# A two-layer hybrid attention and state-space block: the order of fetches and of the first products in the opening

## The chip, the cores and the metric

The kernel runs on one core of a Trainium2 chip. The metric is the device time of one execution in microseconds (us). The engines named below are PE (TensorE, matrix products and transposes), DVE (VectorE), ACT (ScalarE), POOL (GpSimd) and SP (SyncE, which only issues DMAs).

## The reference, cut to what matters

Two layers are applied to 1024 latent tokens and 256 context tokens of width 1024. Only the head of the first layer is touched by the change:

```python
mod = silu(c) @ w_mod[l] + b_mod[l]              # six vectors of 1024: shift, scale, gate, twice
h  = rms_norm(x, norm1_g) * (1 + sc1) + sh1      # and the same for the context with c_ctx
... = split(h @ w_in)                            # q, kv, z, xbc, dt, window q/k/v
```

The rest of a layer is a latent attention, a bidirectional state-space scan, a windowed attention, an output product, and a gated MLP. The scan takes `ssm_dt_bias`, `ssm_a_log` and `ssm_d`, and the windowed attention takes `swa_sink`. These are the scan and sink parameters of the change; each is a handful of numbers that is spread over 128 partitions.

## The kernel before, in words

Everything is kept as features by tokens: `x[f]` holds 128 features (block f of 8) for 1280 tokens. The tokens come in three chunks, 0 and 1 of 512 latent tokens and 2 of 256 context tokens. Every float32 product is split in a high and a low part of each operand (`wh`, `wl` of a weight; `hhi`, `hlo` of the normed input), so that one product of a block with a weight is three matmuls; the first weight has only 64 columns and takes two, so the three first weights together take eight matmuls per block and chunk.

The opening (`start`, from line 1783) does these things for layer 0:

- `fetch(q)` (line 1793) loads the rows of chunk q, one 512 KB DMA for 128 tokens. `turn(q, ...)` (line 1824) transposes them on PE into `x`, 4 transposes for a block of a 512-token chunk, with a copy out of PSUM on DVE or ACT alternately. `stat(q)` takes the mean squares on ACT, and `spread(q, dg)` multiplies them out over the partitions on PE into `pn`.
- `mods(0, (n,), ...)` (line 303) makes 512 columns of `c @ w_mod`; columns 0 and 2 serve the first half of the features (blocks 0 to 3), columns 1 and 3 the second half (blocks 4 to 7). Each column loads four 512 KB pieces `wm` (line 317), does 16 matmuls into `pm`, copies it out (`ev`, line 368), transposes it (`pt`) and reduces it to `modT` (lines 374 and 376). It is a generator that is advanced by hand: the first `next` issues its four loads, two more do the matmuls, the last one the rest.
- `load_params(0, ...)` (line 260) loads ten small parameter arrays as rows (`ra`, `rb`), on ACT's queue, then transposes them on PE (`pa`) into `prm`, and loads five broadcasts `sm` on POOL's queue (lines 281 to 286). Setup puts two more small DMAs of ones (`kpd`, `oned`, line 250) on POOL's queue. `load_params(1, ...)` does the same later in the program for layer 1, all on POOL's queue.
- `apply(q, half)` (line 1832, and `Norm.apply`, line 2105) norms and modulates four blocks of a chunk: for an even block DVE, ACT, DVE; for an odd block DVE, ACT, ACT, POOL.
- `first` (line 695) does the products of the three first weights. It walks six stretches, (chunk, blocks) = (0, 0 to 1), (0, 2 to 3), (1, 0 to 1), (1, 2 to 3), (0, 4 to 7), (1, 4 to 7), and calls `ahead(n)` before the n-th. The context chunk's products follow (`proj2`). The accumulators of the six sums of chunks 0 and 1 are five PSUM buffers of tag `f` (there are five) and one of tag `b` (three); `turn` takes an `f` for chunks 0 and 1, a `b` for chunk 2.

PE runs exactly in program order (`manual_schedule`, line 1950), and so the order of the calls above is the order of its work. The other engines and the DMA queues are ordered at compile time by a scheduler with a priority in program order; `tc.issue_after(ins)` forces what is traced in it behind `ins` on the same queue. Work of the `bg` kind is interleaved with a lower priority.

After the opening all eight `x[f]` are spilled to HBM (`xsp`, line 1980) and the pool that held them is closed. A new pool takes its memory, in which the background generator `mods_v` (line 336) makes the eight other columns of `c @ w_mod` on DVE: 16 instructions and two reductions a column. Its `wm` loads (line 347) can start only when the memory of the `x[f]` under them is free. The program then waits for that generator (`self.drain()` in `body`) before it goes on with the scan.

The lines that carry the order of the opening before:

```python
        dgs = {0: stat(0)}
        next(m[0]); fetch(1); next(m[2])
        turn(0, range(KT)); spread(0, dgs[0])
        next(prm, None); next(m[0]); next(m[0])
        dgs[1] = stat(1); turn(1, range(KT)); spread(1, dgs[1])
```

Of the kernel before, what the change touches and what calls it, by code (L numbers as in the profile page):

```python
# [9 lines left out]
F32 = mybir.dt.float32  # L10
# [9 lines left out]
KT = D // 128  # L20
# [3 lines left out]
NCH = NT // 128  # L24
# [90 lines left out]
class Emit:  # L115
# [92 lines left out]
    def setup(self):  # L208
        nc, tc, ctx = self.nc, self.tc, self.ctx
        self.C = ctx.enter_context(tc.tile_pool(name="const", bufs=1))  # L210
        self.DR = ctx.enter_context(tc.tile_pool(name="dram", bufs=1, space=DRAM))
        c = self.C
        self.ident = c.tile([128, 128], F32, name="ident")
        make_identity(nc, self.ident)
        self.identr = c.tile([128, 128], F32R, name="identr")
        nc.vector.tensor_copy(self.identr, self.ident)
        self.identb = c.tile([128, 128], BF16, name="identb")
        nc.vector.tensor_copy(self.identb, self.ident)
        self.ones = c.tile([128, 128], F32, name="ones")
        nc.vector.memset(self.ones, 1.0)  # L220

        self.negF = c.tile([128, 128], F32, name="negF")
        self.negB = c.tile([128, 128], F32, name="negB")
        for d, t in enumerate((self.negF, self.negB)):
            self.tri(t, d)
            nc.vector.tensor_scalar(out=t, in0=t, scalar1=-1.0, scalar2=-NEG, op0=ALU.add, op1=ALU.mult)

        self.mprev = c.tile([128, 128], BF16, name="mprev")
        self.mnext = c.tile([128, 128], BF16, name="mnext")
        nc.vector.tensor_copy(self.mprev, self.negF)  # L230
        nc.vector.tensor_copy(self.mnext, self.negB)
        self.eps = c.tile([128, 1], F32, name="eps")
        nc.vector.memset(self.eps, EPS)
        dr = lambda name, shape, dt=F32: self.DR.tile(shape, dt, name=name)
        self.spill = dr("xsp", [KT, 128, NT])
        self.fmd = dr("fmd", [NCH, 128, 7, 128])
        self.tmd = dr("tmd", [NCH, 128, 5, 128])
        self.zd = dr("zd", [NCH, 128, 3, 128])
        self.hbd = dr("hbd", [NCH, 128, 384])
        self.gd = dr("gd", [NF, 128, NT])  # L240
        self.ybd = dr("ybd", [3, 128, NT])
        self.acsd = dr("acsd", [12, NCH, 128])
        self.kd = [[dr(f"kd{i}{p}", [128, NT]) for p in range(2)] for i in range(3)]
        self.qd = [[dr(f"qd{i}{p}", [128, NT]) for p in range(2)] for i in range(3)]
        self.swd = [dr(f"swd{i}", [128, NT]) for i in range(4)]
        self.shd = {i: [dr(f"shd{i}{p}", [128, NT]) for p in range(2)] for i in (0, 2, 3)}
        self.kpd = [dr(f"kpd{p}", [33 - p, NT]) for p in range(2)]
        self.oned = dr("oned", [1, NT])
        for d in (self.kpd[0][32:33, :], self.oned):
            nc.gpsimd.dma_start(out=d.rearrange("o (a b) -> (o a) b", b=128), in_=self.ones[0:NCH, :])  # L250
        self.qpd = [[dr(f"qpd{t}{p}", [32 if t == 0 else 128, NT]) for p in range(2)] for t in range(2)]
        self.modd = [[dr(f"modd{l}_{p}", [4, 2, 16, 128]) for p in range(3)] for l in range(DEPTH)]

# [5 lines left out]

    def load_params(self, l, wtile):  # L260
        nc, I = self.nc, self.I
        q = nc.scalar if l == 0 else nc.gpsimd
        prm = self.C.tile([128, PC_ALL], F32, name=f"prm{l}")
        ra, rb = wtile([PC_A, 128], "ra"), wtile([PC_ALL - PC_A, 128], "rb")
        r = lambda ap: ap.rearrange("(f p) -> f p", p=128)
        for o, n, src in ((PC_N1, 8, r(I['norm1_g'][l])), (PC_N2, 8, r(I['norm2_g'][l])),
                          (PC_QN, 2, r(I['mla_q_norm_g'][l])), (PC_KVN, 1, r(I['mla_kv_norm_g'][l])),
                          (PC_CW, 21, I['ssm_conv_w'][l].rearrange("k (f p) -> (k f) p", p=128)),
                          (PC_CB, 7, r(I['ssm_conv_b'][l])), (PC_SN, 3, r(I['ssm_norm_g'][l])), (PC_BM, 48, r(I['b_mod'][l]))):
            q.dma_start(out=ra[o:o + n, :], in_=src)  # L270
        q.dma_start(out=rb[0:66, :], in_=I['ffn_conv_w'][l].rearrange("k (f p) -> (k f) p", p=128))
        q.dma_start(out=rb[66:88, :], in_=r(I['ffn_conv_b'][l]))
        self.prm.append(prm)
        sm = self.C.tile([128, 12 + 12 + 4 + 3], F32, name=f"sm{l}")
        self.small.append(sm)
        yield 15.0
        pa = self.b("pa")
        self.tr(pa[:, 0:PC_A], ra)
        self.tr(pa[:, PC_A:PC_ALL], rb)
        nc.vector.tensor_copy(prm, pa[:, 0:PC_ALL])  # L280
        nc.gpsimd.dma_start(out=sm[:, 0:12], in_=I['ssm_dt_bias'][l].rearrange("a b -> (a b)").partition_broadcast(128))
        nc.gpsimd.dma_start(out=sm[:, 12:24], in_=I['ssm_a_log'][l].rearrange("a b -> (a b)").partition_broadcast(128))
        nc.gpsimd.dma_start(out=sm[:, 24:28], in_=I['swa_sink'][l].partition_broadcast(128))
        dsk = I['ssm_d'][l].rearrange("(i two) -> two i", two=2)
        for hf in range(2):
            nc.gpsimd.dma_start(out=sm[64 * hf:64 * hf + 64, 28:31], in_=dsk[hf].partition_broadcast(64))


    def mod_stat(self):
# [1493 lines left out]
    def start(self):  # L1783

        nc, I, tc = self.nc, self.I, self.tc
# [7 lines left out]
        def fetch(q):  # L1793
            for k in range(CHUNKS[q][0] // 128, CHUNKS[q][1] // 128):
                rows[k] = self.u(shape=[128, D], name="xr")
                nc.sync.dma_start(out=rows[k], in_=row(k))
# [10 lines left out]
        def stat(q):  # L1807
            s, e = CHUNKS[q]
            k0, k1 = s // 128, e // 128
            sp = lambda w, name: self.u(shape=[128, w], name=name) if q else self.W.tile([128, D], F32, tag="wlo", name=self.nm(name))  # L1810
            junk, dg = sp(D, "junk"), sp(512, "dg")
            for k in range(k0, k1):
                nc.scalar.activation(junk, rows[k], AF.Square, accum_out=st[:, k:k + 1])
            self.rsqrt(r[:, k0:k1], st[:, k0:k1], D)
            self.diag(dg, r[:, k0:k1], k1 - k0)
            return dg
# [7 lines left out]
        def turn(q, fs):  # L1824
            s, e = CHUNKS[q]
            for f in fs:
                p = self.b("ptr") if q == 2 else self.f("ptr")
                for k in range(s // 128, e // 128):
                    self.tr(p[:, k * 128 - s:k * 128 - s + 128], rows[k][:, f * 128:(f + 1) * 128])
                (nc.scalar.copy if f % 2 or q == 2 else nc.vector.tensor_copy)(x[f][:, s:e], p[:, 0:e - s])  # L1830
# [5 lines left out]
            norm.apply(CHUNKS[q], pn[:, s:e], [4 * hf + f for f in fs])  # L1836

        norm.halves = set()
        prm = self.load_params(0, xw)
        next(prm)  # L1840
        dgs = {0: stat(0)}
        next(m[0])
        fetch(1)
        next(m[2])
        turn(0, range(KT))
        spread(0, dgs[0])
        next(prm, None)
        next(m[0])
        next(m[0])
        dgs[1] = stat(1)  # L1850
        turn(1, range(KT))
        spread(1, dgs[1])
        with tc.issue_after(self.last_w.ins):
            for i in range(3):
                self.wready.append(self.wload(*self.wspec.pop(0), pool=i == 2, stage=self.X.tile([128, KT, 128], F32, tag="ft", name=self.nm("w")) if i == 2 else None))
        next(m[0], None)
        next(m[2])
        next(m[2])
        next(m[2], None)
        for q in range(2):  # L1860
            apply(q, 0)
        next(m[1])
        next(m[3])
        with tc.issue_after(self.last_w.ins):
# [2 lines left out]
        def ahead(i):  # L1867

            if i == 2:
                for n in (1, 3):  # L1870
                    next(m[n])
                    next(m[n])
                dgs[2] = stat(2)
            if i == 3:
                for n in (1, 3):
                    next(m[n], None)
                apply(0, 1)
                turn(2, range(KT))
                spread(2, dgs[2])
                with tc.issue_after(self.last_w.ins):  # L1880
                    self.wready.append(self.wload(*self.wspec.pop(0), tile=lambda sh, tag, name: self.u(F32R, sh, name)))
                    self.wprime(2)
            if i == 4:
                apply(1, 1)
                apply(2, 0)
                apply(2, 1)
        return x, (norm.hi, norm.lo), ahead
# [339 lines left out]
```

## Time and profile before

| | |
|---|---|
| median of 3 runs | 3299.73 us (3297.24 to 3301.19) |
| the profiled execution, its own time | 3301.97 us |
| span from the first to the last instruction in it | 3300.3 us |
| mean granted TensorE clock | 0.957 of full |
| busy: PE, DVE, ACT, POOL | 93%, 65%, 39%, 19% of the span |
| DMA | 392 MB, mean 119 GB/s |

The profile is that of one execution, with the time of each instruction, what it waited for, and when each DMA landed. Times in it count from the start of the span. A row of a timeline gives the start, the length, the engine, the line, the operation, and what it writes and reads; an idle time before it stands in brackets with what ended it. "SPq" is SP's queue, where a DMA's row is its issue and not its transfer. The first 220 us, 6.7% of the span, are the part that the change touches.

### The profile page before, as it was taken

The numbers are of one execution on the slowest core, as the hardware profiler recorded it, in microseconds if no ns is written. First come the engines' busy times: TensorE is split into PE (matmuls) and PEld (weight loads), VectorE is DVE, ScalarE is ACT, GpSimd is POOL, SyncE is SP. The second block draws the span as 40 slices with busy tenths as digits, with TensorE's granted clock in tenths as the row PEclk, the third lists the DMA queues.
The fourth block names the chain that finished last, engine by engine and source line by source line (L and its number), as shares of the span: only waits on it lengthen the run. The fifth ranks groups of instructions, "written<-read, shape, count | busy, mean of one in ns | idle before, by whom it ended". The sixth has DMA issues, their size and how long they took to land.

```text
span 3300.3 us, 40044 instructions
## 1 busy us (share of the span) xinstructions
PE 3067.8 (93%) x15321; PEld 2408.6 (73%) x15321; DVE 2145.1 (65%) x3172; ACT 1275.9 (39%) x2203; POOL 614.6 (19%) x382
## 2 busy tenths in 40 slices
PE   7989878997989999997999999889999899999998
PEld 4878755554868888886888788755557678887887
DVE  5985887665385566558865634878563767776544
ACT  5334543343263343342211543543342544444212
POOL 2104633444100000000000303544452000000001
PEclk9989988998999999998999999888999999999999
DMA  8765665102202212236652345754113122225321
GB/s 266 231 185 150 213 217 155 40 14 96 93 29 71 79 59 71 77 102 242 198 157 67 129 117 160 226 179 122 41 52 102 45 77 87 85 83 185 112 74 64
DMA packets 348160, 392.42 MB, mean 119 GB/s; under 512 B 37138, under 2 KB 274339, under 8 KB 347968
## 3 DMA queue, kind: packets, MB, share of 16 engines
q1 hardware_dynamic: 347004, 389.62, 37.5%
q8 instruction: 121, 1.98, 0.2%
q0 software_dynamic: 704, 0.14, 0.1%
q14 instruction: 71, 0.58, 0.1%
q10 hardware_dynamic: 260, 0.10, 0.0%
HBM read 284.48 MB, written 104.01 MB: 118 GB/s over the span
## 4 chain that ended last, share of the span: by engine, by line
PE 76%; DVE 14%; DMA 5%; issue 2%; ACT 2%; POOL 1%; SPq 0%; DVEq 0%; ACTq 0%; POOLq 0%
PE p L143 33%; PE X L143 10%; PE Z L143 7%; PE s L143 6%; PE py L143 5%; PE pc L143 4%; PE V L143 3%; PE Y L143 3%; DVE wm L354 2%; DVE mx L1362 1%; DMA gr<-gd 1%; PE pm L143 1%; DVE hb L2153 1%; PE pn L143 1%; PE pst L143 1%
## 5 line engine op out<-in xcount | busy, mean ns | idle before, releaser
L143 PE MATMUL p<-gh,wb 128*128 128x512 f32 (+1 forms) x1760 | 508.2, 372 | 20.5 <-ACT gh L1744 20.5
L436 ACT CAST wb<-w 128x512 fp32r<-128x512 f32 x411 | 254.0, 622 | 571.4 <-PE p L143 282.3
L437 DVE TENSOR_TENSOR wb<-w,wb 128x512 fp32r<-128x512 f32 x411 | 281.2, 689 | 260.6 <-ACT wb L436 256.4
L143 PEld LDWEIGHTS p<-gh,wb 128*128 128x128 f32 x1760 | 322.4, 190 | 79.5 <-ACT gh L1744 23.8
L143 PE MATMUL X<-hb,wb 128*128 128x512 f32 x1512 | 360.4, 391 | 9.5 <-ACT hb L2152 4.6
L1572 DVE SCALAR_TENSOR_TENSOR x<-p,modT,x 128x512 f32<-128x512 f32 (+1 forms) x280 | 193.4, 695 | 231.9 <-PE p L143 231.6
L143 PEld LDWEIGHTS X<-hb,wb 128*128 128x128 f32 x1512 | 284.8, 189 | 70.9 <-ACT hb L2152 5.3
L143 PE MATMUL p<-gl,wb 128*128 128x512 f32 (+1 forms) x880 | 327.2, 372 | 2.6 <-DVE gl L1745 2.6
L143 PE MATMUL p<-hhi,wh 128*128 128x512 f32 (+1 forms) x792 | 292.6, 377 | 5.4 <-ACT z L648 3.1
L143 PE MATMUL p<-hlo,wh 128*128 128x512 f32 (+3 forms) x792 | 290.9, 368 | 1.9 <-DVE hlo L2123 1.0
L143 PE MATMUL p<-hhi,wl 128*128 128x512 f32 (+1 forms) x744 | 273.3, 367 | 3.6 <-DVE wl L424 3.1
L143 PE MATMUL Z<-hb,wb 128*128 128x512 f32 x1008 | 245.8, 393 | 8.7 <-ACT wb L436 4.4
L1446 ACT ACTIVATE P<-s 128x512 f32<-128x512 f32 x240 | 142.5, 598 | 239.9 <-PE s L143 234.1
L2075 POOL TENSOR_TENSOR acc<-acc,sq 128x512 f32<-128x512 f32 x24 | 32.9, 1374 | 1042.8 <-ACT sq L2074 1042.5
L143 PEld LDWEIGHTS Z<-hb,wb 128*128 128x128 f32 x1008 | 189.1, 189 | 49.4 <-ACT wb L436 4.6
L1453 POOL TENSOR_TENSOR acc<-acc,P 128x1024 f32<-128x1024 f32 x69 | 168.9, 2448 | 189.1 <-ACT P L1446 169.9
L143 PEld LDWEIGHTS p<-gl,wb 128*128 128x128 f32 x880 | 167.1, 190 | 32.8 <-DVE gl L1745 5.1
L143 PEld LDWEIGHTS p<-hhi,wh 128*128 128x128 f32 x792 | 152.1, 193 | 32.0 <-ACT z L648 4.0
L143 PE MATMUL py<-P,vt 128*64 128x512 f32 (+3 forms) x744 | 174.3, 584 | 0.0
L354 DVE SCALAR_TENSOR_TENSOR wm<-wm,mstat,wm 128x512 f32<-128x512 f32 x224 | 161.3, 752 | 19.8 <-DMA wm<-in_w_mod_dram 19.2
L143 PEld LDWEIGHTS p<-hlo,wh 128*128 128x128 f32 (+1 forms) x792 | 150.2, 190 | 25.4 <-DVE hlo L2123 1.7
L143 PEld LDWEIGHTS p<-hhi,wl 128*128 128x128 f32 x744 | 143.0, 192 | 28.4 <-DVE wl L424 4.4
(396 smaller groups left out, 5947.7 us busy)
## 6 DMA issues: line engine op xcount, KB each, us to landing
wm<-in_w_mod_dram SPq DMA_DIRECT2D x96, 512.0 KB
w<-in_ffn_w_up_dram SPq DMA_DIRECT2D x88, 512.0 KB
w<-in_ffn_w_down_dram SPq DMA_DIRECT2D x44, 512.0 KB
w<-in_w_in_dram SPq DMA_DIRECT2D x30, 512.0 KB
gd<-ft SPq DMA_DIRECT2D x22, 640.0 KB
gr<-gd SPq DMA_DIRECT2D x22, 640.0 KB
ab<-acsd SPq DMA_DIRECT2D x36, 384.0 KB
tm<-tmd SPq DMA_DIRECT2D x38, 320.0 KB
```

Source lines behind the costliest of these rows:

```text
L143: self.nc.tensor.matmul(out=out, lhsT=lhsT, rhs=rhs, start=start, stop=stop, **kw)
L354: nc.vector.scalar_tensor_tensor(out=acc[:, v, :], in0=w[:, i, :], scalar=c, in1=acc[:, v, :], op0=ALU.mult, op1=ALU.add)
L436: self.nc.scalar.copy(t[:, 0], raw)
L437: self.nc.vector.tensor_sub(t[:, 1], raw, t[:, 0])
L1362: nc.vector.tensor_reduce(out=m[:, j, s:s + 1], in_=p, axis=AXX, op=ALU.max)
L1446: nc.scalar.activation(P[:, q * 512:(q + 1) * 512], s, AF.Exp, scale=sc)
L1453: (nc.vector if kt in ((2, 4, 6, 8) if self.scan else (4, 7)) else nc.gpsimd).tensor_add(acc, acc, P)
L1572: self.nc.vector.scalar_tensor_tensor(out=t[:, s:e], in0=p[:, 0:e - s], scalar=self.mcol(l, v, m)[:, o:o + 1], in1=t[:, s:e], op0=ALU.mult ...
L2075: (nc.gpsimd if self.n[ch] < 6 else nc.vector).tensor_add(acc, acc, sq[:, :n])
L2153: nc.vector.tensor_sub(lo, raw, hi)
```

## The change

Setup no longer loads `kpd` and `oned`; layer 0's small parameters go on SP's queue in place of ACT's, and its five broadcasts wait behind a second `yield` and go on SP's queue too. In the opening, columns 0 and 2 are fetched directly behind chunk 0; then come the small parameters, the three first weights, and only then chunk 1. Chunk 1 is turned, and its first half normed, in `ahead(2)`, that is behind the products of chunk 0 with blocks 0 to 3. Columns 1 and 3 are finished in `ahead(4)`, the context chunk is turned in `ahead(5)`, and the five broadcasts, `kpd` and `oned` are issued there.

```diff
-        for d in (self.kpd[0][32:33, :], self.oned):
-            nc.gpsimd.dma_start(out=d.rearrange("o (a b) -> (o a) b", b=128), in_=self.ones[0:NCH, :])
...
-        q = nc.scalar if l == 0 else nc.gpsimd
+        q = nc.sync if l == 0 else nc.gpsimd
...
         nc.vector.tensor_copy(prm, pa[:, 0:PC_ALL])
-        nc.gpsimd.dma_start(out=sm[:, 0:12], in_=I['ssm_dt_bias'][l]...)
+        if l == 0:
+            yield
+        q.dma_start(out=sm[:, 0:12], in_=I['ssm_dt_bias'][l]...)
...
-        prm = self.load_params(0, xw)
-        next(prm)
         dgs = {0: stat(0)}
         next(m[0])
-        fetch(1)
         next(m[2])
+        prm = self.load_params(0, xw)
+        with tc.issue_after(self.last_w.ins):
+            next(prm)
+            for i in range(3):
+                self.wready.append(self.wload(...))
+            fetch(1)
         turn(0, range(KT))
         spread(0, dgs[0])
         next(prm, None)
-        next(m[0])
-        next(m[0])
-        dgs[1] = stat(1)
-        turn(1, range(KT))
-        spread(1, dgs[1])
-        with tc.issue_after(self.last_w.ins):
-            for i in range(3):
-                self.wready.append(self.wload(...))
-        next(m[0], None)
-        next(m[2])
-        next(m[2])
-        next(m[2], None)
-        for q in range(2):
-            apply(q, 0)
+        def columns(ns):
+            for n in ns:
+                next(m[n])
+                next(m[n])
+                next(m[n], None)
+        columns((0, 2))
+        apply(0, 0)
         next(m[1])
         next(m[3])
         with tc.issue_after(self.last_w.ins):
             fetch(2)
         def ahead(i):
             if i == 2:
-                for n in (1, 3):
-                    next(m[n])
-                    next(m[n])
+                dgs[1] = stat(1)
+                turn(1, range(KT))
+                spread(1, dgs[1])
+                apply(1, 0)
+            if i == 4:
+                columns((1, 3))
+                apply(0, 1)
                 dgs[2] = stat(2)
-            if i == 3:
-                for n in (1, 3):
-                    next(m[n], None)
-                apply(0, 1)
+                apply(1, 1)
+            if i == 5:
                 turn(2, range(KT))
                 spread(2, dgs[2])
                 with tc.issue_after(self.last_w.ins):
                     self.wready.append(self.wload(...))
                     self.wprime(2)
-            if i == 4:
-                apply(1, 1)
+                    next(prm, None)
+                    for d in (self.kpd[0][32:33, :], self.oned):
+                        nc.sync.dma_start(out=d.rearrange("o (a b) -> (o a) b", b=128), in_=self.ones[0:NCH, :])
                 apply(2, 0)
                 apply(2, 1)
```

## Rows read from the trace of the kernel before

**Rows 1.** The chain of waits, 190 to 235 us: shares by line

```profile
by line: DVE wm L354 39.5%; PE p L143 21.0%; DVE xbc L508 10.7%; issue 8.9%; DVE modT L361 5.3%; DVE wl L424 5.1%; PE pt L148 4.3%; PE pdt L148 2.7%; DVE wm L352 1.8%; PE pa L148 0.7%; DVE modT L362 0.5%; DVE a L390 0.3%; DVE edge L516 0.1%
```

**Rows 2.** Busy time by stretch: stretch, length, PE, PEld, DVE, ACT, POOL, PEclk, DMA share, GB/s

```profile
0.00:10.00 10.00, 1.23 (x3) 0.54 (x3) 1.62 (x10) 1.48 (x2) 6.76 (x18) 1.00 0.74 178
10.00:20.00 10.00, 4.47 (x20) 4.17 (x21) 1.45 (x3) 4.85 (x9) 1.49 (x3) 1.00 0.74 195
20.00:30.00 10.00, 7.62 (x36) 3.61 (x35) 3.23 (x6) 7.22 (x14) 0.00 (x0) 0.83 0.96 345
...
100.00:120.00 20.00, 20.00 (x105) 17.13 (x104) 20.00 (x28) 5.12 (x6) 6.42 (x3) 1.00 0.75 220
...
200.00:220.00 20.00, 8.95 (x51) 7.67 (x49) 20.00 (x38) 7.51 (x10) 5.20 (x10) 0.74 0.54 165
```

**Rows 3.** Timeline of VectorE, 60 to 140 us: start, us, instruction, idle before it

```profile
76.35 0.47 DVE L2120 SCALAR_TENSOR_TENSOR nt<-x,a,pn 128x256 f32<-128x256 f32 x1
...
84.19 0.41 DVE L2126 TENSOR_TENSOR nt<-x,pn 128x256 f32<-128x256 f32 x1
...
88.04 0.88 DVE L352 TENSOR_SCALAR wm<-wm,mstat 128x512 f32<-128x512 f32 x2 [1.12 <-DMA wm<-in_w_mod_dram]
```

**Rows 4.** Timeline of SP's queue, 0 to 120 us

```profile
62.41 9.30 SPq L1980 DMA_DIRECT2D xsp<-x  x8
...
84.29 0.38 SPq L347 DMA_DIRECT2D wm<-in_w_mod_dram  x1
```

**Rows 5.** Timeline of TensorE, 14 to 41 us

```profile
16.01 6.25 PE L148 MATMUL ptr<-ident,xr 128*128 128x128 f32 x29 [4.46 <-DMA xr<-in_x_dram]
23.98 1.12 PE L143 MATMUL pn<-dg,ones 128*128 128x512 f32 x2 [1.72 <-DVE dg L403]
...
25.03 0.24 PE L148 MATMUL pa<-ident,rb 88*128 88x88 f32 x1
25.20 3.56 PE L143 MATMUL pm<-wm,mstat 128*32 128x512 f32 x16
...
29.91 3.39 PE L148 MATMUL ptr<-ident,xr 128*128 128x128 f32 x29 [0.67 <-DMA xr<-in_x_dram]
...
34.86 1.92 PE L143 MATMUL pm<-wm,mstat 128*32 128x512 f32 x16
37.72 0.63 PE L148 MATMUL pt<-ident,ev 128*128 128x128 f32 x4 [0.93 <-DVE ev L368]
40.57 0.50 PE L143 MATMUL p<-hhi,wh 128*128 128x512 f32 x1 [2.23 <-ACT hhi L2122]
```

**Rows 6.** The chain of waits, 0 to 110 us, in order of time

```profile
46.26 7.10 PE p L143 x24
...
77.53 7.58 PE p L143 x32
```

**Rows 7.** SP's waits, 0 to 100 us: total, times, longest

```profile
SPq L317 <- DMA xr<-in_x_dram: 11.4, 4, 4.6
```

**Rows 8.** DMA queues, 0 to 200 us: packets, MB, share of 16 engines

```profile
q0 software_dynamic: 384, 0.04, 2.2%
```

**Rows 9.** Timeline of POOL, 0 to 14 us

```profile
1.37 0.76 POOL L281 DMA_DIRECT2D sm<-in_ssm_dt_bias_dram  x1 [0.36 <-issue]
...
6.36 0.58 POOL L281 DMA_DIRECT2D sm<-in_ssm_dt_bias_dram  x1
```

**Rows 10.** Busy time by stretch, columns as above, 26 to 28 us

```profile
26.00:28.00 2.00, 2.00 (x16) 0.39 (x8) 0.00 (x0) 1.95 (x4) 0.00 (x0) 0.50 1.03 409
```

**Rows 11.** Timeline of all engines, 46 to 50 us: one odd block of a normed half

```profile
46.68 0.68 DVE L2126 TENSOR_TENSOR nt<-x,pn 128x512 f32<-128x512 f32 x1
...
47.39 0.82 ACT L2127 ACTIVATE nt<-nt,modT,a 128x512 f32<-128x512 f32 x1 [1.56 <-DVE nt L2126]
...
48.24 0.62 ACT L2128 CAST hhi<-nt 128x512 fp32r<-128x512 f32 x1
...
48.94 1.50 POOL L2129 TENSOR_TENSOR hlo<-nt,hhi 128x512 fp32r<-128x512 f32 x1 [2.73 <-ACT hhi L2128]
```

More of the change, by code (lines that the diff above doesn't have):

```diff
@@ L280, in load_params @@
         nc.vector.tensor_copy(prm, pa[:, 0:PC_ALL])
-        nc.gpsimd.dma_start(out=sm[:, 0:12], in_=I['ssm_dt_bias'][l].rearrange("a b -> (a b)").partition_broadcast(128))
-        nc.gpsimd.dma_start(out=sm[:, 12:24], in_=I['ssm_a_log'][l].rearrange("a b -> (a b)").partition_broadcast(128))
-        nc.gpsimd.dma_start(out=sm[:, 24:28], in_=I['swa_sink'][l].partition_broadcast(128))
+        if l == 0:
+            yield
+        q.dma_start(out=sm[:, 0:12], in_=I['ssm_dt_bias'][l].rearrange("a b -> (a b)").partition_broadcast(128))
+        q.dma_start(out=sm[:, 12:24], in_=I['ssm_a_log'][l].rearrange("a b -> (a b)").partition_broadcast(128))
+        q.dma_start(out=sm[:, 24:28], in_=I['swa_sink'][l].partition_broadcast(128))
         dsk = I['ssm_d'][l].rearrange("(i two) -> two i", two=2)
         for hf in range(2):
-            nc.gpsimd.dma_start(out=sm[64 * hf:64 * hf + 64, 28:31], in_=dsk[hf].partition_broadcast(64))
+            q.dma_start(out=sm[64 * hf:64 * hf + 64, 28:31], in_=dsk[hf].partition_broadcast(64))
     def mod_stat(self):
@@ L1838, in start @@
         norm.halves = set()
-        prm = self.load_params(0, xw)
-        next(prm)
         dgs = {0: stat(0)}
         next(m[0])
-        fetch(1)
         next(m[2])
+        prm = self.load_params(0, xw)
+        with tc.issue_after(self.last_w.ins):
+            next(prm)
+            for i in range(3):
+                self.wready.append(self.wload(*self.wspec.pop(0), pool=i == 2, stage=self.X.tile([128, KT, 128], F32, tag="ft", name=self.nm("w")) if i == 2 else None))
+            fetch(1)
         turn(0, range(KT))
@@ L1847, in start @@
         next(prm, None)
-        next(m[0])
-        next(m[0])
-        dgs[1] = stat(1)
-        turn(1, range(KT))
-        spread(1, dgs[1])
-        with tc.issue_after(self.last_w.ins):
-            for i in range(3):
-                self.wready.append(self.wload(*self.wspec.pop(0), pool=i == 2, stage=self.X.tile([128, KT, 128], F32, tag="ft", name=self.nm("w")) if i == 2 else None))
-        next(m[0], None)
-        next(m[2])
-        next(m[2])
-        next(m[2], None)
-        for q in range(2):
-            apply(q, 0)
+        def columns(ns):
[5 more added lines that the diff above has]
+        apply(0, 0)
         next(m[1])
```

## The prediction

> **What bounds the kernel now.** The change touches the first 220 us alone, so I looked first for what ends that stretch. The chain of waits around its end is mostly DVE's: `mods_v`'s multiply-adds hold 39.5% of it [rows 1]. The busy times say the same: DVE is busy without a gap from 100 to 120 us and again from 200 to 220, where PE has fallen to 8.95 of 20 us because the program drains the background generator [rows 2]. So the end of the stretch is the start of `mods_v` plus a fixed amount of DVE work. That start is at 88.04 us, when its first `wm` has landed [rows 3]; the load was issued at 84.29 [rows 4], as the last normed blocks of the context chunk were read (84.19 [rows 3]). Hence the rule of this sum: **a us by which the last reading of `x` moves is a us of the whole kernel**, and nothing that happens earlier counts unless it moves that.
>
> Before that point two things rule. Up to 40.57 us, the first product [rows 5], it is the DMAs: they moved only 178 and 195 GB/s in the first two stretches of 10 us [rows 2], against 409 when nothing disturbed them [rows 10]. From then on it is PE's fixed order with little idle time: 24 products at 46.26 and 32 at 77.53 are single pieces of the chain [rows 6].
>
> 0.2% of the time, 6.6 us, is about what a measurement of this kernel can tell from no change.
>
> **The early fetches.** Before the first product the program now needs chunk 0, columns 0 and 2, the small parameters and three weights; chunk 1, 2.1 MB, moves behind them. When has the last piece of column 2 landed? It is the twelfth of 512 KB, 6.3 MB. At 409 GB/s from 2.2 us on that is 17.6 us; on the present curve (1.78 MB by 10 us, 1.95 more by 20, then 345 GB/s [rows 2]) it is 27.4. Two losses make the difference. The broadcasts on POOL's queue took 2.2% of 16 engines for 200 us, 4.4 us of each [rows 8]; half of that goes, because POOL issues layer 1's five directly behind layer 0's (6.36 against 1.37 us [rows 9]) and will issue them even sooner. And SP stood still for 11.4 us over four issues, each until one of the `xr` had landed [rows 7], though they don't share a buffer; I read that as a limit on DMAs in flight which ACT's ten small ones now help to fill. I take 22 us, near the middle, since one loss is halved and the other shrinks.
>
> The ten parameters queue behind that on SP. By the same limit the last three can be issued only once column 2 has landed: 1 us of issuing and 2 of latency (between nothing and 2.4, the 3.75 us of a lone `wm` from issue to use [rows 3, 4] less 1.3 for its data). So the parameters are there at 25 us. The Trainium skill, in "DMA: Bandwidth & Descriptors", section "Issuing engines are not separate DMA queues", says that all queues share the same 16 engines and that another issuing engine saves only the sequencer's time, usually small beside the transfer. By that the move to SP would cost nothing, and the sum below would be 3 us smaller; the 11.4 us of waiting in SP's own order speak against it here.
>
> **From the parameters to the first product.** On PE `pa` stands ahead of column 0, so all that follows waits for the parameters. `pa` takes 0.3 (0.24 for the second [rows 5]). Column 0 took 3.56 us for 16 matmuls with the granted clock at 0.50, its 1.2 GHz level, after PE had stood still before and behind the sums of chunk 0; column 2 took 1.92 at 2.4 GHz [rows 5, 10]. PE will again come from waiting, so 3.5 for the first. From the start of column 2's matmuls to the end of its transposes it was 3.5 us (34.86 to 38.35 [rows 5]); with no work between, both columns now run one after the other: 5.1 + 3.5. Then 2.2 from 38.35 to the first product at 40.57 [rows 5]. Sum: 25 + 0.3 + 5.1 + 3.5 + 2.2 = **36.1**, 4.5 us earlier than now. Three weights follow the parameters on SP and are there before that: they are 1.3 MB.
>
> **From the first product on.** A stretch of 32 products takes 7.58 us [rows 6]. An odd block's low part needs 0.68 + 0.82 + 0.62 + 1.50 on four engines in a row [rows 11], some 4.4 after `pn` as its first step waits behind the even block's, while the first even block is ready at 1.5 and its eight products take 1.9. So where PE comes straight from `pn`, it waits 1.0 for the second block: 8.6 for 32 products, and 10.1 from `pn`. Today this stall is paid once; three times now, since the norm of each half stands directly ahead of its products.
>
> - Chunk 0, blocks 0 to 3: 36.1 + 8.6 = 44.7. Now that end is 53.4 (46.26 + 7.10 [rows 6]): 8.7 gained.
> - Chunk 1 is turned there, in place of before the first product. It takes 3.39 with five PSUM buffers free, 6.25 for chunk 0 beside ACT's statistics [rows 5]. Three of the five `f` buffers now hold sums, so two are left: I take 4.8, the middle. Then `spread` 1.12 [rows 5] and a copy of 0.6: 51.2.
> - Chunk 1, blocks 0 to 3: 10.1, to 61.3.
> - Columns 1 and 3, one after the other: 3.5 each, 7.0, to 68.3. They now cost PE about that less 2 x 0.9 waiting for `ev`, beside products.
> - `modT`, and chunk 0, blocks 4 to 7: 2.2 to the first product, then 8.6, to 79.1. The second half of chunk 1 is normed under it.
> - The context is turned: half of 4.8, `spread` 1.0, to 82.5.
> - Its norm: 8.2 as now (76.35 to 84.60 [rows 3]), to **90.7** against 84.6.
>
> The last reading of `x` is then **6.1 us later**. What was gained at the start (8.7) is spent on turning chunk 1 behind the first products (6.5, which lay under the fetches before), on stalls on `pn` and `modT` that were filled with other products (about 6), and on `ev` (2).
>
> What is late next: the spill of `x` needs the turned context. Today its eight issues begin at 62.41 [rows 4], 22 us before the memory is wanted. In the new order they begin at about 80, and 5.24 MB at 409 GB/s are 12.8 us, so until 93; the first `wm`, issued at 91, would land at 94.2 anyway (91 + 3.75, less rounding). I add nothing, but 0 to 3 us is the bound if `wm` queues behind the spill.
>
> Costed at nothing: the five broadcasts, `kpd` and `oned` on SP (seven issues of some 0.4 us in a queue that is idle there, for values that are read after 200 us); the later second half of the parameters; statistics of chunk 1 on ACT, which waits for PE then. If ACT's order at compile time puts these ahead of a norm, up to 5 us come on top.
>
> Sum: 3299.7 + 6.1 = **3306** against the median; against the profiled execution's 3301.97, which stands 2.2 above the median, 3308.
>
> **The rivals.**
>
> - *The fetches run free, faster.* With POOL's and ACT's small DMAs out of the way the queue runs at 409 GB/s from the start: column 2 at 17.6, parameters at 20.6, column 0 at full clock, first product 30.1. With the short ends after it too (no stall of 1.0 three times, 3.4 and 1.7 for turning, 6 for the last norm, which is 7.3 in all) the last reading comes at 77.4, 7.2 earlier: 3292.5. For it: the 409. Against it: layer 1's broadcasts stay. It decides from a first product below 30.7 with all short ends, or 23.4 with none.
> - *The gain is eaten exactly.* The first product comes at 36, and the scheduler fills half of the stalls: 3300 to 3303.
> - *The spill holds the generator up, much slower.* Its 12.8 us follow the turned context on SP, and `wm` waits behind them, with ACT late besides: 3310 to 3315. For it: SP's order; against it: the norm of the context takes most of that time anyway.
> - *It doesn't do what it says.* Layer 1's broadcasts, and the cold start of the fetches, keep the present curve: column 2 at 27.4, first product at 41.5, and the whole sum 5.4 higher: 3311.
>
> **How the numbers follow.** Forecast, 3302 to 3310: 0.44. Free fetches: 0.24. Eaten: 0.16. Spill: 0.09. Unchanged curve: 0.07. The forecast lies just inside the 6.6 us, with 0.20 of its 0.44 within and 0.24 above. So faster by over 0.2%: 0.24; within: 0.16 + 0.20 = 0.36; slower: 0.24 + 0.09 + 0.07 = 0.40. The range from 3292 to 3315 takes in the free fetches' end and the spill; the forecast's own is 3302 to 3310.
>
> **What would show it.** Right: the first product at 34 to 38 us behind a wait of PE for `ra` or `rb`; 32 transposes behind the first 32 products; columns 1 and 3 each with an idle gap before `pt`; eight `xsp` issued from 78 to 84; `mods_v`'s first instruction at 93 to 96, and DVE without a gap from there to the drain. Wrong: that instruction before 85, or PE not waiting between `modT` and the products behind it, or a difference that arises after 230 us, where only the scheduler's order could have changed.

## The result, and the profile after

The changed kernel takes **3335.7 us** in the median of 4 runs (3332.1 to 3337.6), against 3300.3 for the kernel before on the same chip: a ratio of 1.0113 (95% interval 1.0101 to 1.0126), 35 us slower. The forecast was 3306, with 3315 as the end of its range. The profiled execution's span is 3330.4 us, 30.1 more than before; 3332.09 was its own time. The medians are 35 us apart and the two profiled executions 30: the changed kernel's is the fastest of its four, and that of before, at 3301.97, is slower than the four that make its median.

Where do the 30 us arise? VectorE's timeline has the first instruction of `mods_v`, which was at 88.04 us [rows 3]:

```profile
118.20 0.93 DVE L352 TENSOR_SCALAR wm<-wm,mstat 128x512 f32<-128x512 f32 x2 [1.72 <-DMA wm<-in_w_mod_dram]
```

It comes 30.2 us later, and the span is 30.1 longer. The busy times by stretch (columns as in [rows 2]) show that the fixed DVE work lies behind it almost without a gap (18.73 of 20 us from 120 to 140, then 20.00 in each stretch up to 240), and ends in the stretch from 240 us on. Before, it ended in the stretch from 220 on. The rows of the changed kernel come first, then that one of before:

```profile
10.00:20.00 10.00, 4.42 (x20) 4.13 (x21) 1.77 (x4) 4.84 (x8) 0.00 (x0) 1.00 0.91 315
20.00:30.00 10.00, 4.25 (x20) 2.75 (x22) 2.03 (x4) 1.76 (x3) 0.00 (x0) 0.75 0.51 165
...
38.00:41.00 3.00, 3.00 (x16) 0.50 (x16) 1.07 (x2) 0.00 (x0) 1.10 (x1) 0.50 1.03 399
...
220.00:240.00 20.00, 16.98 (x97) 14.32 (x96) 20.00 (x38) 8.64 (x13) 0.00 (x0) 1.00 0.80 232
240.00:260.00 20.00, 9.78 (x38) 8.00 (x39) 15.65 (x31) 4.57 (x7) 5.18 (x10) 0.50 0.56 178
```

```profile
220.00:240.00 20.00, 17.92 (x79) 14.93 (x80) 11.78 (x35) 4.37 (x6) 0.00 (x0) 0.75 0.39 126
```

So the rule of the prediction held in this pair of executions, and the loss lies ahead of 118.20. SP's queue shows the fetches (the first number is the issue, the second how long the group took to issue):

```profile
3.43 13.38 SPq L317 DMA_DIRECT2D wm<-in_w_mod_dram  x8
17.38 1.65 SPq L268 DMA_DIRECT2D ra<-in_norm_g_dram  x2
20.10 0.23 SPq L268 DMA_DIRECT2D ra<-in_mla_q_norm_g_dram  x1
...
26.70 0.32 SPq L268 DMA_DIRECT2D ra<-in_b_mod_dram  x1
...
27.86 2.56 SPq L413 DMA_DIRECT2D w<-in_w_in_dram  x4
30.46 2.77 SPq L1796 DMA_DIRECT2D xr<-in_x_dram  x4
```

From 20.10 to 26.70 six of the small parameters go out, one per 1.3 us. SP's waits say for what:

```profile
SPq L268 <- DMA wm<-in_w_mod_dram: 7.9, 8, 1.1
```

Eight times SP waited for a `wm` to land before it could issue one of these small loads, and the weights and chunk 1 stood behind. With nothing large issued behind the `wm`, the transfers ran dry: 377 GB/s from 20 to 21 us, 6 from 26 to 27. TensorE's timeline is where the rest is read:

```profile
28.77 0.40 PE L148 MATMUL pa<-ident,ra 98*128 98x98 f32 x1 [5.75 <-DMA rb<-in_ffn_conv_w_dram]
...
29.46 3.11 PE L143 MATMUL pm<-wm,mstat 128*32 128x512 f32 x16
36.89 1.08 PE L148 MATMUL pt<-ident,ev 128*128 128x128 f32 x4 [4.32 <-DVE ev L368]
37.90 3.64 PE L143 MATMUL pm<-wm,mstat 128*32 128x512 f32 x16
...
45.27 0.57 PE L143 MATMUL p<-hhi,wh 128*128 128x512 f32 x1 [2.23 <-ACT hhi L2124]
...
55.43 1.04 PE L148 MATMUL ptr<-ident,xr 128*128 128x128 f32 x8
...
62.01 1.13 PE L143 MATMUL pn<-dg,ones 128*128 128x512 f32 x2 [1.16 <-DVE dg L403]
65.35 0.49 PE L143 MATMUL p<-hhi,wh 128*128 128x512 f32 x1 [2.22 <-ACT hhi L2124]
67.13 0.69 PE L143 MATMUL p<-hlo,wh 128*64 128x512 f32 x1 [1.28 <-DVE hlo L2125]
...
77.03 1.92 PE L143 MATMUL pm<-wm,mstat 128*32 128x512 f32 x16
...
86.82 0.69 PE L143 MATMUL p<-hlo,wh 128*64 128x512 f32 x1 [3.01 <-DVE hlo L2125]
...
96.31 0.60 PE L148 MATMUL ptr<-ident,xr 128*128 128x128 f32 x4
...
102.67 1.22 PE L143 MATMUL pn<-dg,ones 128*128 128x256 f32 x2 [0.32 <-ACT x L1830]
```

The 4.32 us ahead of `pt` are explained by VectorE's timeline: column 0's matmuls ended at 32.57, but its copy `ev` stood behind a weight's split that waited for ACT's cast, and this for the weight's transfer:

```profile
34.92 1.23 DVE L424 TENSOR_TENSOR wl<-w,wh 128x1024 fp32r<-128x1024 f32 x1 [1.69 <-ACT wh L423]
36.06 0.68 DVE L368 COPY ev<-pm 128x512 f32<-128x512 f32 x1
```

The order on PE is the one that the prediction expected, with the waits that it named, but most are longer, and one is of a kind that it did not price: the context chunk is turned from 96.31 on, and its `pn` is copied out only at 106.62. ACT's timeline tells why:

```profile
101.64 0.58 ACT L654 COPY krdt<-p 44x512 f32<-44x512 f32 x1
...
102.63 1.28 ACT L648 ACT_TABLE_LOAD   x1
103.93 0.60 ACT L648 ACTIVATE z<-p 128x512 f32<-128x512 f32 x1
...
105.42 1.04 ACT L423 CAST wh<-w 128x1024 fp32r<-128x1024 f32 x1
106.35 0.38 ACT L1830 COPY x<-ptr 128x256 f32<-128x256 f32 x1
106.62 0.40 ACT L1822 COPY pn<-pn 128x256 f32<-128x256 f32 x1
```

The evictions of the finished sums (`krdt`, `z`), a table load and a weight's cast stand ahead of the last copy of `x` and of `pn`. Before, the context was turned and normed ahead of those products, and so ahead of their evictions: its `pn` was copied at 66.48, the first `krdt` at 85.62. The last reading of `x`, on VectorE, now ends at 116.48:

```profile
115.64 0.84 DVE L2128 TENSOR_TENSOR nt<-x,pn 128x256 f32<-128x256 f32 x1
```

### The profile page after: what moved, and what is told of

Same layout as the page of the kernel before. It is cut to its first block, busy times and chain, and to the rows that moved or that the text cites. A ratio compares the mean times of both kernels' runs of the same rounds, so it can differ in the third digit from the quotient of the medians.

```text
span 3330.4 us, 40037 instructions
## 1 busy us (share of the span) xinstructions
PE 3080.1 (92%) x15321; PEld 2415.6 (73%) x15321; DVE 2146.0 (64%) x3172; ACT 1275.9 (38%) x2204; POOL 606.3 (18%) x375
## 4 chain that ended last, share of the span: by engine, by line
PE 68%; DVE 10%; DMA 2%; issue 1%; ACT 1%; POOL 1%; SPq 0%; DVEq 0%; ACTq 0%; POOLq 0%
PE p L143 28%; PE X L143 10%; PE Z L143 6%; PE s L143 5%; PE py L143 4%; PE pc L143 3%; PE V L143 3%; PE Y L143 3%; DVE mx L1362 1%; DMA gr<-gd 1%; DVE hb L2155 1%; PE pm L143 1%; PE pn L143 1%; PE pd L143 1%; DVE acc L1397 1%
## 5 line engine op out<-in xcount | busy, mean ns | idle before, releaser
L143 PEld LDWEIGHTS Z<-hb,wb 128*128 128x128 f32 x1008 | 190.3, 191 | 49.3 <-ACT wb L436 4.6
```

Of the source, the lines that this page charges most:

```text
L143: self.nc.tensor.matmul(out=out, lhsT=lhsT, rhs=rhs, start=start, stop=stop, **kw)
```

## The experiments

Theory T, formed on these rows: most of the loss lies between the first product and `mods_v` and comes from the new order of products. Rival R1: it comes from the late fetches. T expects a short stretch wherever the order of before is kept, R1 wherever the fetches are early. Each run was timed beside the kernel before on the same chip (medians 3297.4, 3297.4 and 3296.8 in the three groups).

### The two halves of the change, and two of its fetch parts

**Fetches alone.** All edits to fetches, parameters and broadcasts; the order of products of before:

```diff
-        columns((0, 2))
-        apply(0, 0)
+        next(m[0]); next(m[0])
+        dgs[1] = stat(1); turn(1, range(KT)); spread(1, dgs[1])
+        next(m[0], None)
+        next(m[2]); next(m[2]); next(m[2], None)
+        for q in range(2):
+            apply(q, 0)
...
```

> The changed fetches, parameters and broadcasts, with the order of products of before (chunk 1 turned before the first product). Theory T (most of the 30 us is lost between the first product and mods_v, by the new order of products): the first product comes at 45 to 48 us, because chunk 1 is now fetched last and is again needed first; from there to mods_v's first instruction 47.5 us as before, so that instruction at 93 to 96 and the time 3305 to 3309. Rival R1 (the loss is in the late fetches and in what ACT and DVE have to do late because of them): mods_v at 110 or later, time 3322 or more.

Measured: 3310.2, ratio 1.0041 (1.0026 to 1.0055). The first product was later than expected, since PE now waited for chunk 1 and three times for single pieces of it; TensorE's timeline, then VectorE's:

```profile
38.31 0.45 PE L148 MATMUL ptr<-ident,xr 128*128 128x128 f32 x1 [4.57 <-DMA xr<-in_x_dram]
...
53.91 0.49 PE L143 MATMUL p<-hhi,wh 128*128 128x512 f32 x1 [2.23 <-ACT hhi L2127]
```

```profile
100.48 0.88 DVE L352 TENSOR_SCALAR wm<-wm,mstat 128x512 f32<-128x512 f32 x2 [1.11 <-DMA wm<-in_w_mod_dram]
```

From 53.91 to 100.48 are 46.6 us, against 47.5 before: the latest first product of all, in the order of before, cost 13 us and not 30. Time and `mods_v` lie a little above T's ranges and far below R1's.

**Order alone.** `columns`, the late turns and norms, and `apply(0, 0)` only; every fetch issued as before:

```diff
-        dgs[1] = stat(1); turn(1, range(KT)); spread(1, dgs[1])
...
+        columns((0, 2))
+        apply(0, 0)
...
             if i == 2:
+                dgs[1] = stat(1); turn(1, range(KT)); spread(1, dgs[1])
+                apply(1, 0)
+            if i == 4:
+                columns((1, 3))
...
```

> The changed order of products alone; fetches, parameters and broadcasts issued as before. T: the first product at 38 to 41 us, from there to mods_v's first instruction about 73 us as in the changed kernel, so that instruction at 111 to 114 and the time 3322 to 3327. R1: the stretch shrinks back towards 50 us once the fetches are early, mods_v at 88 to 95, time 3300 to 3307.

Measured: 3327.1, ratio 1.0088 (1.0073 to 1.0103). First product at 40.63, as before; `mods_v` at 118.99, 78 us later and 5 beyond T's range. That order alone brings 30 us (24 in the profiled pair), the fetches alone 13; together they come to 42, against 35 for both, and each is known to some 5 us. T stands, and R1 falls as the main cause.

**Broadcasts alone.** The five broadcasts, `kpd` and `oned` late on SP, the rest as before:

```diff
+        if l == 0:
+            yield
+        q = nc.sync if l == 0 else nc.gpsimd
-        nc.gpsimd.dma_start(out=sm[:, 0:12], ...)
+        q.dma_start(out=sm[:, 0:12], ...)
...
```

> The kernel before, with layer 0's five broadcasts, kpd and oned issued late on SP's queue; nothing else. T: half of the small packets of POOL's queue leave the first 50 us, first product 0 to 3 us earlier than 40.57, mods_v 0 to 3 us earlier, time 3297 to 3300. R1 would have the same or more: that the broadcasts on POOL are what slows the fetches, 3293 to 3297. If the late issues on SP get in the way of the scan: over 3302.

Measured: 3299.0, ratio 1.0003 (0.9994 to 1.0012). The fetches did get faster, with 160 packets on POOL's queue in place of 384; the busy times of 10 to 20 and 20 to 30 us have 258 and 394 GB/s where they were 195 and 345 [rows 2]:

```profile
10.00:20.00 10.00, 4.20 (x19) 3.91 (x20) 1.38 (x2) 4.58 (x9) 0.00 (x0) 1.00 0.80 258
20.00:30.00 10.00, 8.15 (x43) 4.38 (x42) 3.48 (x7) 8.59 (x15) 0.00 (x0) 0.83 1.02 394
```

But the first product came at 39.94 and `mods_v` at 87.55, 0.6 and 0.5 us earlier, as T had it: the opening hardly waited for what those packets held up.

**Parameters back on ACT's queue**, at the start; the rest as changed:

```diff
-        q = nc.sync if l == 0 else nc.gpsimd
+        q = nc.scalar if l == 0 else nc.gpsimd
...
+        prm = self.load_params(0, xw)
+        next(prm)
         dgs = {0: stat(0)}
...
```

> The changed kernel, with the ten small parameter arrays on ACT's queue at the start as before. T: PE's pa no longer waits (it waited 5.75 us at 28.77), first product at 37 to 39 in place of 45.27, and the stretch behind it stays 70 to 73: mods_v at 108 to 112, time 3320 to 3326. R1: with the parameters early ACT and DVE are clear and nearly all is won back, 3306 or less.

Measured: 3324.8, ratio 1.0080 (1.0063 to 1.0098). TensorE's timeline:

```profile
34.44 0.80 PE L143 MATMUL p<-hhi,wh 128*128 128x512 f32 x1 [2.23 <-ACT hhi L2124]
...
55.83 1.13 PE L143 MATMUL pn<-dg,ones 128*128 128x512 f32 x2 [3.24 <-DVE dg L404]
```

The first product is 10.8 us earlier than in the changed kernel, and the time 10.9 less (1.0113 less 1.0080 of 3300). So moving the parameters to SP's queue, behind the `wm`, cost some 11 us, more than their own lateness (which part is the queue's and which the later place was not tried). In the profiled executions `mods_v` moved by 6.8 only, and this one is the slowest of its four (3320.0 to 3329.6). `mods_v` and time are in T's ranges, far from R1's 3306. Yet with a first product 6 us *earlier than before*, the kernel is 27 us slower: 77 us lie between it and `mods_v` (111.43).

### The waits between the first product and `mods_v`

These start from the last kernel and move one thing at a time. R2: the pace of DVE and ACT sets the end, whatever the order.

**The context turned earlier:**

```diff
             if i == 4:
                 columns((1, 3))
-                apply(0, 1)
                 dgs[2] = stat(2)
-                apply(1, 1)
-            if i == 5:
                 turn(2, range(KT))
                 spread(2, dgs[2])
+                apply(0, 1)
+                apply(1, 1)
+            if i == 5:
```

> The kernel with parameters on ACT's queue (e4_params_on_act, 3324.8), with the context chunk's statistics, transposes and spread moved from behind the products of chunk 0 with blocks 4 to 7 to ahead of the norm of those blocks. There they took 10.7 us of PE (89.17 to 99.87), most of it waiting for copies that stand behind other work in ACT's order. Theory T (three waits of PE's fixed order make up the loss, of which this is the largest): they take 3 to 5 us, under the wait of 3.0 us for the first normed block, so mods_v 6 to 8 us earlier and the time 3316 to 3319. Rival R2 (the later norms themselves, on ACT, DVE and POOL, set the end whatever PE does): the end of the norms moves by less than 2 us, time 3322 to 3327.

Measured: 3316.8, ratio 1.0056 (1.0041 to 1.0071), 8.0 less. The turn and spread took 4.7 us. The time is in T's range; `mods_v` came at 107.19, 4.2 earlier where T had 6 to 8. VectorE's timeline showed the next wait:

```profile
94.75 1.22 DVE L425 TENSOR_TENSOR wl<-w,wh 128x1024 fp32r<-128x1024 f32 x1 [3.79 <-ACT wh L424]
95.89 1.48 DVE L2122 SCALAR_TENSOR_TENSOR nt<-x,a,pn 128x256 f32<-128x256 f32 x1
```

The context's norm (95.89), whose `pn` was there at 81, is behind a weight's split that waits for ACT.

**The context normed earlier, too:**

```diff
                 apply(1, 1)
+                apply(2, 0)
+                apply(2, 1)
             if i == 5:
...
-                apply(2, 0)
-                apply(2, 1)
```

> e5_context_turn_earlier (3316.8) with the context chunk's norm, too, traced ahead of the products of chunk 0 with blocks 4 to 7, where before had it, in place of behind them. Theory T2 (formed on e5: behind those products the norm stands on ACT and DVE behind the evictions of z and krdt, the table load and a weight's cast, and DVE is idle for 10 of the 27 us from the spread to mods_v): mods_v's first instruction from 107.2 to 98 to 100, the 21.8 us from the spread on that before has; time 3307 to 3311. Rival R2 (the norms come at the pace of DVE and ACT in any order): mods_v at 105 or later, time 3314 to 3318.

Measured: 3319.9, ratio 1.0071 (1.0057 to 1.0085). VectorE's timeline:

```profile
99.86 0.88 DVE L353 TENSOR_SCALAR wm<-wm,mstat 128x512 f32<-128x512 f32 x2 [1.88 <-DMA wm<-in_w_mod_dram]
```

`mods_v` came as T2 says, 7.3 us earlier, which R2 excluded, but the time is no less and lies above both ranges. Here the rule broke, after the drain, as the prediction had listed among what would make it wrong. ACT's table loads serve as marks; in layer 1 two of them were at 2055.05 and 2213.05 before, and are here at

```profile
2063.47 1.28 ACT L958 ACT_TABLE_LOAD   x1
2228.44 1.28 ACT L399 ACT_TABLE_LOAD   x1
```

that is 8.4 late at the first and 15.4 at the second. The stretch between them is 7 us longer, at a lower granted clock; first the kernel before (2055 to 2213), then this one:

```profile
2055.00:2213.00 158.00, 133.93 (x809) 105.63 (x809) 123.73 (x194) 82.77 (x206) 76.90 (x50) 0.90 0.62 193
```

```profile
2063.00:2229.00 166.00, 140.32 (x813) 108.82 (x813) 132.72 (x194) 84.13 (x207) 76.39 (x51) 0.87 0.59 185
```

DVE is busy for 9 us more, but that is not it: with the fetches alone it is busy for 132.30 between the same marks, and they are 156.5 us apart. In the profiled executions of all thirteen kernels the stretch takes 155.8 to 165.0 us, at a granted clock of 0.94 in the shortest and 0.87 in the longest, this one. Which of the two follows from the other, and why this kernel is at the end of the row, stays open.

**Statistics of chunk 1 earlier:**

```diff
         columns((0, 2))
+        dgs[1] = stat(1)
         apply(0, 0)
...
             if i == 2:
-                dgs[1] = stat(1)
```

> The same kernel as e4_params_on_act with the statistics of chunk 1 traced ahead of the first product in place of behind the products of chunk 0; PE's order is unchanged. T: PE's wait of 3.24 us for dg before spread goes to under 0.6, and nothing else changes: time 3320.5 to 3323. R2: the wait moves into the norm of chunk 1 behind it, time 3324 to 3326.

Measured: 3323.9, ratio 1.0081 (1.0066 to 1.0096): nothing won that can be told. The wait for `dg` went (the spread at 56.86 has none), and another came, which neither theory had put there. ACT's timeline, VectorE's, and then TensorE's:

```profile
33.67 1.06 ACT L1814 ACTIVATE junk<-xr 128x1024 f32<-128x1024 f32 x1 [0.24 <-DMA xr<-in_x_dram]
```

```profile
39.08 0.18 DVE L400 RECIPROCAL rst<-rst 128x4 f32<-128x4 f32 x1 [1.84 <-ACT rst L399]
...
39.90 0.74 DVE L2122 SCALAR_TENSOR_TENSOR nt<-x,a,pn 128x512 f32<-128x512 f32 x1
```

```profile
41.45 0.80 PE L143 MATMUL p<-hhi,wh 128*128 128x512 f32 x1 [7.68 <-ACT hhi L2124]
```

The statistics now wait for chunk 1's rows on ACT, their last steps on DVE wait for ACT, and the first norm (`nt`) stands behind these: the first product is 7 us later.

**Three waits out at once:** the edits of the context's turn and of the statistics, and the matmuls of columns 1 and 3 one stretch of products earlier:

```diff
+            if i == 3:
+                for n in (1, 3):
+                    next(m[n])
+                    next(m[n])
             if i == 4:
-                columns((1, 3))
+                for n in (1, 3):
+                    next(m[n], None)
...
```

> e4_params_on_act with both edits of e5 and e6, and with the matmuls of columns 1 and 3 one stretch of products earlier, so that their copies lie beside products. T: the three waits add up, 7 + 3 + 2 to 4 us: mods_v at 97 to 100, time 3310 to 3314; what is left to before is turning chunk 1 behind products (about 6) and the stalls on pn. R2: no better than e5 and e6 alone, 3318 or more.

Measured: 3319.0, ratio 1.0060 (1.0043 to 1.0076). A miss for T: the three don't add up, because the statistics again delay the first product (41.23, behind 6.65 us of waiting). `mods_v` at 107.72. The time lies where R2 had it, but R2's reason does not hold: with the context's norm moved, `mods_v` did come earlier (above).

**Chunk 1 turned between the first two stretches of products**, on top of the context's turn and norm:

```diff
-            if i == 2:
+            if i == 1:
                 dgs[1] = stat(1)
                 turn(1, range(KT))
...
```

> e8_context_norm_earlier with chunk 1 turned, and its first half normed, one stretch of products earlier (behind chunk 0 with blocks 0 to 1). T: the norm of chunk 1 then lies under the products of chunk 0 with blocks 2 to 3, so PE's waits of 2.3 and 0.9 us for it go, and part of the wait of 3.2 for dg: mods_v 3 to 6 us earlier than in e8, time 3303 to 3307. R3 (ACT's order puts the statistics ahead of chunk 0's norm, as in e6): the first product waits for that norm, and the time is that of e8 within 2 us, or above it.

Measured: 3311.7, ratio 1.0043 (1.0029 to 1.0057), 8.3 less, but not as T says: `mods_v` came at 100.81, a us later than in its parent, and the spread waited 6.59 us for `dg` in place of 3.24. That is neither T's time nor R3's. In the profiled executions the gain is the loss in layer 1, which this one does not have: the same two table loads are at 2063.11 and 2221.36, 158 us apart as before.

### Versions in the order of before

**Chunk 1 turned between column 2 and the first product**, `ahead` of before, parameters on ACT's queue and early columns:

```diff
         columns((0, 2))
-        apply(0, 0)
+        dgs[1] = stat(1)
+        turn(1, range(KT))
+        spread(1, dgs[1])
+        for q in range(2):
+            apply(q, 0)
...
```

> Fetches as in e4_params_on_act, but chunk 1 turned between the second column and the first product, and everything behind it in the order of before. T: the turn (3.4 to 5 us) fills PE's wait for modT and the first norm; first product at 36 to 39 without stalls behind it, the stretch to mods_v at most the 47.5 us of before, so that instruction at 82 to 87 and the time 3291 to 3298: no slower than before, and faster if chunk 1 lands by 34 us. R1 (late weights and fetches): the first product waits for chunk 1 beyond 41 us, time over 3301.

Measured: **3294.5**, ratio 0.9988 (0.9978 to 0.9997), the fastest here; but the first product was at 43.63, beyond R1's 41, as the turn waited for chunk 1's rows (33.56 to 37.41), and `mods_v` at 87.31, only 0.7 us earlier than before. The time is T's, the first product R1's. Its interval lies below 1, but the lead of 3 us is within the 0.2% that the prediction set as the limit of what can be told, and where it arises is not settled. Between the kernel above (14.8 us slower than before) and this one lie chunk 1's turn and norm, the place of columns 1 and 3 and that of the context: how the 17.7 us divide among them was not tried.

**The same with chunk 1 fetched before the weights:**

```diff
         with tc.issue_after(self.last_w.ins):
+            fetch(1)
             for i in range(3):
                 self.wready.append(self.wload(...))
-            fetch(1)
```

> e10_turn_before_products (3294.5) with chunk 1 fetched ahead of the three first weights. In e10 the turn of chunk 1 waited for its rows from 33.56 to 37.4 us. T: the rows come 3 us earlier, the weights as much later; the first product at 39 to 41 in place of 43.6, mods_v at 83 to 85, time 3290 to 3293. R1 (the DMAs' sum sets the first product, whatever their order): the first product waits for a weight's cast, at 42 or later, time 3294 to 3297.

Measured: 3294.8, ratio 0.9989 (0.9978 to 0.9999). The turn now ran in one piece and the first product came at 38.67; the next had to wait. TensorE's timeline, then VectorE's:

```profile
33.96 3.66 PE L148 MATMUL ptr<-ident,xr 128*128 128x128 f32 x32
...
38.67 0.50 PE L143 MATMUL p<-hhi,wh 128*128 128x512 f32 x1 [0.20 <-ACT hhi L2128]
43.07 0.69 PE L143 MATMUL p<-hlo,wh 128*64 128x512 f32 x1 [3.89 <-DVE hlo L2129]
```

```profile
38.99 1.21 DVE L425 TENSOR_TENSOR wl<-w,wh 128x1024 fp32r<-128x1024 f32 x1
40.12 0.68 DVE L1831 COPY x<-ptr 128x512 f32<-128x512 f32 x1
40.72 2.29 DVE L2129 SCALAR_TENSOR_TENSOR hlo<-nt,modT,hhi 128x512 fp32r<-128x512 f32 x1
```

DVE had the copies of chunk 1 and the weights' splits to do first, and `hlo` itself took 2.29 us, against 0.75 in the changed kernel (45.25). `mods_v`: 87.94, as before; T had 83 to 85.

### All runs together

| kernel | first product, us | from there to `mods_v` | `mods_v` against before | time against before |
|---|---|---|---|---|
| before | 40.57 | 47.5 | 0 | 0 |
| changed | 45.27 | 72.9 | +30.2 | +35.4 |
| fetches alone | 53.91 | 46.6 | +12.4 | +12.7 |
| order alone | 40.63 | 78.4 | +31.0 | +29.7 |
| broadcasts alone | 39.94 | 47.6 | -0.5 | +1.6 |
| parameters on ACT | 34.44 | 77.0 | +23.4 | +27.4 |
| + context turned earlier | 34.05 | 73.1 | +19.2 | +19.5 |
| + context normed earlier, too | 34.55 | 65.3 | +11.8 | +23.1 |
| + chunk 1 turned between, too | 34.51 | 66.3 | +12.8 | +14.8 |
| parameters on ACT + statistics earlier | 41.45 | 71.1 | +24.5 | +26.6 |
| three waits out | 41.23 | 66.5 | +19.7 | +21.7 |
| turned before products | 43.63 | 43.7 | -0.7 | -2.9 |
| chunk 1 before weights | 38.67 | 49.3 | -0.1 | -2.0 |

Time against before is the difference of the medians. But for one kernel it follows `mods_v` within 6 us. The spans of the profiled executions follow it within 7.3 us in all twelve (worst in the order alone: 23.7 for 31.0), so a difference of a few us between two of these kernels can't be read from `mods_v` alone. The first product tells nothing: at 34.5 the kernel is 15 to 27 us slower than before, at 43.6 it is level or faster.

## Why the prediction was wrong

The direction was right, and so was the rule that ties the time to the last reading of `x`. The rest was not: the gain of 4.5 us at the start was a loss of 4.7 (first product at 45.27, against 40.57), at the end of the first 32 products it was a loss of 2.1 (55.43 against 53.36) in place of 8.7 gained, and some of the waits behind it were not in the sum at all. Its sum, step by step, with the measured times of the changed kernel (from TensorE's, VectorE's and ACT's timelines):

| step | predicted | measured | off by |
|---|---|---|---|
| first product | 36.1 | 45.27 | +9.2 |
| chunk 0, blocks 0 to 3 | 8.6 | 10.2 (to 55.43) | +1.6 |
| turn, spread and copy of chunk 1 | 6.5 | 8.3 (to 63.76) | +1.8 |
| chunk 1, blocks 0 to 3 | 10.1 | 13.3 (to 77.03) | +3.2 |
| columns 1 and 3 | 7.0 | 6.8 (to 83.81) | -0.2 |
| `modT`; chunk 0, blocks 4 to 7 | 10.8 | 12.5 (to 96.31) | +1.7 |
| turn, spread and copy of the context | 3.4 | 10.7 (to 107.02) | +7.3 |
| its norm | 8.2 | 9.5 (to 116.48) | +1.3 |

- **The rule** that a us of the last reading of `x` is a us of the kernel: right here. The prediction's 6.1 and the 25.8 of the table are 31.9; 1.7 came back as the first `wm` was there sooner behind the last reading (118.20 less 116.48, against 88.04 less 84.60). That gives 30.2, the shift of `mods_v`.
- **"So the parameters are there at 25 us"**: wrong by 3.8 (`pa` at 28.77). Column 2, put at 22 us, had landed only by 26.7, when the last wait for a `wm` ended. One of the two losses did shrink: 315 GB/s from 10 to 20 us, against 195. The other, SP standing still until a transfer lands, moved more than it shrank: before, the loads of `wm` waited 11.4 us for the `xr`; now the rows of the parameters waited 7.9 us for the `wm`, eight times up to 1.1, and from 20 to 30 us the queues moved 165 GB/s. The rest of the 9.2: `pa` took 0.4 longer; from column 0's first matmul to column 2's it was 8.4 us in place of 5.1, since `ev` stood behind the weight's split on DVE; and column 2, after that wait of PE, ran at the 1.2 GHz level (granted clock 0.50 from 38 to 41 us) and took 5.1 to the end of its `pt` (43.04) in place of 3.5. The 2.2 behind it held. With the parameters on ACT's queue at the start `ev` stood behind no split, both columns took 1.92 us, and the first product was at 34.44: all three went with the parameters.
- **The Trainium skill**, "DMA: Bandwidth & Descriptors", section "Issuing engines are not separate DMA queues", by which another issuing engine matters little: the prediction set SP's waits against it, and was right to, but priced them at 3 us. SP waited 7.9 us before it could issue eight loads of at most 24 KB. The run with the parameters on ACT's queue (and first in program order) measured 10.9; as it changed the place too, it does not price the issuing engine by itself.
- **"half of 4.8, `spread` 1.0" for the context**: the step behind the first product that failed most, by 7.3 us. It counted PE's matmuls and not the engine that empties their PSUM. ACT makes all these copies, and its order had `krdt`, a table load, two `z` and a weight's cast among them. Moving the turn ahead of those products gave 8.0 us of the time (4.2 of `mods_v`); moving the norm too brought `mods_v` another 7.3 forward.
- **"Costed at nothing: [...] statistics of chunk 1 on ACT"**: wrong in the changed kernel by 1.2 us (the wait for `dg`), by 3.2 with the parameters early. The prediction named the danger (statistics ahead of a norm, up to 5 us); the run that moved them there had its first product 7 us later.
- **The stalls on `pn`**: 1.0 for each of three were meant to cover them. Chunk 1's first product waited 2.22 us for `hhi` and its first low part 1.28 more, and the products behind ran at the 1.2 GHz level at first (granted clock 0.50 from 66 to 72 us). Blocks 4 to 7 waited 3.01 us, where 2.2 had been counted, and began at a granted clock of 0.51 (87 to 90 us).
- **The rivals**: "Fetches run free" was closest to its first product of 30.1 in the run with parameters on ACT's queue (34.44), and that was still 27 us slower than before. "The spill holds the generator up" had the right side, but neither the size nor the cause: the eight `xsp` were issued from 97.13 to 107.08 us, and the first `wm` at 114.56, as the last blocks of the context were read. "It doesn't do what it says" was nearly right on column 2: the last parameter that waits for a `wm` went out at 26.70, against its 27.4.

The range failed since nearly all terms were bounded by PE's and the DMAs' rows. For ACT's order the prediction named up to 5 us, for the statistics, and left them out of the sum and the range; for the copies out of PSUM it set nothing, and for `ev` behind the weights on DVE nothing, although [rows 11] showed that both engines are in the chain of every odd block.

## What to carry to other kernels

Work that was moved behind a group of products was moved behind their evictions on ACT too: for each moved step, list what now stands ahead of it on the engine that drains its PSUM, not only on the one that computes it. An earlier first product is worth nothing by itself; measure from the work that sets the end back. Small transfers that the first result needs are better issued where no large transfer stands ahead of them.

## What was unexpected of the hardware

A queue's cost for small transfers: ten small loads behind eight of 512 KB on SP took from 17.4 to 27.8 us to issue, six of them one per 1.3 us, each held until one of the large ones had landed. Whether the queue or the program's own waits hold them is not shown. With them on ACT's queue at the start the kernel was 10.9 us faster. And taking 224 of the 384 small packets of POOL's queue away raised the rate of 10 to 20 us from 195 to 258 GB/s, for no gain in time that could be measured.
